# Where the decay weights and the rank rows of a gated linear attention are made, and which forward preparation comes first

## The chip, the cores and the metric

The kernel runs on one core of a Trainium2 chip, in one launch. The metric is the device time of the launch in microseconds (us). Five engines run their own instruction streams and meet at semaphores: PE (TensorE, matrix products and transposes), DVE (VectorE), ACT (ScalarE), POOL (GpSimd) and SP (SyncE, which here only issues transfers). An engine takes its instructions in the order in which they were written for it; an instruction whose input isn't there holds up all that stand behind it on that engine.

## The reference, cut to what matters

One encoder layer on 1024 tokens with 16 learned meta tokens ahead of them, width 1024. A combined projection feeds two groups of heads: a neighbourhood attention (16 heads of 64 over a 16 x 64 grid, window 8 x 16, meta tokens as extra keys) and a bidirectional gated linear attention (GLA; 4 heads, keys of 128, values of 256, decays per key from a projection of rank 16). Both are gated, put side by side and projected back onto the residual. What the change touches is the decay of the GLA and the meta tokens' part of its forward state:

```python
u = rmsnorm(concat([meta, x]), norm_g)                  # 1040 x 1024
gq, gk, gv, r_f, r_b, g_gate, nq, nk, nv, n_gate = split(u @ w_in)
lg_f = log_sigmoid(r_f @ w_decay_fwd + b_decay_fwd) / 16   # r_f, r_b: 1040 x 16
lg_b = log_sigmoid(r_b @ w_decay_bwd + b_decay_bwd) / 16   # w_decay: 16 x 512
G    = cumsum(lg) within a chunk
q_in, k_in, k_st = q * exp(G), k * exp(-G), k * exp(G_last - G)
U    = k_st^T v                 # per chunk and head: 128 x 256
S    = exp(G_last) * S + U      # state from chunk to chunk, in each direction
o    = tril(q_in k_in^T) v + q_in S
o_gla = rmsnorm(o_f + o_b) * silu(g_gate)
out  = x + concat([o_gla, neighbourhood_attention(...) * silu(n_gate)]) @ w_out
```

## The kernel before, in words

All matrix products that need it are made from three products of rounded halves (`mm3`, L411 to L413: high x high, low x high, high x low), so a dense projection shows as rows of L411, L412, L413 in turn. The channels of a weight row block (`raw`) are split into `wh` and `wl` by ACT, DVE and POOL ahead of PE.

The program is written out in one fixed order by a small planner, `Sched` (L69). It keeps an estimate of PE's time, `S.pe`. The main work is a generator that yields what it needs next: `("w", ns)` adds PE time, `("gap", ns)` fills that much estimated PE time with the next groups of the dense projections (`filler`), and `S.defer(ns, fn)` writes `fn`'s instructions once the estimate has advanced by ns. So a gap's length decides how many matmuls of dense work stand between two steps of the main work, and nothing is decided when the kernel runs.

There are two phases. First, eight head pairs of the neighbourhood attention, `attn(p)` for p = 0 to 7, some 69 us each; the filler brings the projections of the next pair and, late, `dense_gz(0)` and `dense_gv(0)` (queries, keys, values and rank columns of the first GLA head). In the trace `attn(2)` begins near 200 us and `attn(4)` near 338 us. Within `attn` the rows that matter here are: `Q` split into two halves (L731 by ACT, L738 by DVE, L742 by POOL), the scores `s` (L764, L765), softmax's maximum (L792) and exponentials (L798), its division `P` (L812 to L815), the transposes of `P` into `pp` (L826), their copies `PT` (L830 by ACT for the first head, L832 by DVE for the second) and the product with the values, `po` (L845). The natural-layout rows of the next pair come in between: squares and sums (`ss`, L552, by DVE), their inverse roots (`rstd`, L209 and L210, by POOL) and the scaled rows `nat` (L557, by DVE).

Then the attention's pool is closed, a pool `gp` is opened in its place, and the GLA begins: `gla_static()` (L995) reserves and loads constants, `r_prep()` (L917) turns the rank columns `rst` into rows, and `gla(h)` runs for the four heads, with the output gate `gg`, the next head's `gz` and `gv` and finally the output projection as filler. For each head the decays of the backward direction are made first (`decay_pe(1)`, product `pdec` at L1059, and on through ACT and DVE to `ga` and `gm`), then those of the forward direction; then the backward states run from chunk 7 to chunk 1 (transposed keys `pk` L1160, halves `kn` L1162 and L1163, products `pu`, states `SB` L1183 to L1186).

Three things are touched:

- **The decay weights `wd`**, one tile of 128 x 512 for each direction: rows 0 to 63 hold the rounded weights twice, rows 64 to 95 what the rounding left, rows 96 and 97 the bias in two halves, the rest zeros. The raw weights come by four transfers a direction into `wdst` (L1006, L1007); `wd_prep` (L1014) makes each tile by a memset on POOL and four operations on DVE (L1017 to L1021). Both directions are made in one piece in `r_prep`, after its first gap.
- **The rank rows `RS`**, 128 x 1040: transposes of `rst` on PE (`rt`, L929), six copies by ACT (L939), three subtractions by DVE (L941), and two memsets by POOL for the rows that meet the bias (L920, L921). `pdec` is `RS` times `wd`. Behind the three subtractions on DVE stand the evacuations of the gate's first two accumulation banks, `gt` from `pz_gg` (`gate_evac`, L484), which free the banks.
- **The forward preparations** (`fwd`, L1138): six steps that are written one by one behind the backward states of chunks `FWD_AT`: a cumulative sum over 1024 columns (`decay_scan`, L1080), its centring (`decay_mid`, L1088 to L1092), the meta tokens' key product (`ma`, the tile `mt`, L1141), exponentials and two products. The transpose of `ma` on PE, `pkt` (L1191), is written behind chunk 5.

## Time and profile before

| | |
|---|---|
| median of 3 runs | 1161.38 us (1160.01 to 1161.72) |
| the profiled execution's own time | 1161.92 us |
| its span, first to last instruction | 1159.1 us |
| PE busy | 1127.0 us, 97% of the span, 6739 matmuls |
| DVE busy | 771.6 us, 67%, 1965 instructions |
| ACT busy | 531.9 us, 46%, 1377 instructions |
| POOL busy | 300.8 us, 26%, 415 instructions |
| mean granted clock of TensorE | 0.997 |

How to read the rows: in the timeline, the first number is the start in us from the span's start, the second the duration, then engine, source line, operation, output and inputs with their shapes, and in square brackets the idle time just before and what ended it. In the list of waits, each row has an engine and the work that waited, what it waited for, and then the total in us, how many times, and the longest. In the table by stretches, each engine has its busy time and its number of instructions, followed by the granted clock of TensorE (1 is full), the mean busy share of the core's 16 transfer engines and GB/s. A stretch's matmuls are pipelined: a 512-column matmul lasts about 0.40 us in the record, and the next begins some 0.23 us after it began, so PE's pace is read from starts.

### The profile page before, as it was taken

The numbers are of one execution on the slowest core, as the hardware profiler recorded it, in microseconds if no ns is written. First come the engines' busy times: TensorE is split into PE (matmuls) and PEld (weight loads), VectorE is DVE, ScalarE is ACT, GpSimd is POOL, SyncE is SP. The second block draws the span as 40 slices with busy tenths as digits, with TensorE's granted clock in tenths as the row PEclk, the third lists the DMA queues.
The fourth block names the chain that finished last, engine by engine and source line by source line (L and its number), as shares of the span: only waits on it lengthen the run. The fifth ranks groups of instructions, "written<-read, shape, count | busy, mean of one in ns | idle before, by whom it ended". The sixth has DMA issues, their size and how long they took to land.

```text
span 1159.1 us, 18919 instructions
## 1 busy us (share of the span) xinstructions
PE 1127.0 (97%) x6739; PEld 981.4 (85%) x6739; DVE 771.6 (67%) x1965; ACT 531.9 (46%) x1377; POOL 300.8 (26%) x415
## 2 busy tenths in 40 slices
PE   8899999999999999999999799999999999999998
PEld 7789898998989889898898689879978977788886
DVE  6966767677677776767664676675486578656352
ACT  6756565664656555465553342542343244212120
POOL 3753534335353433624323001101100100000000
PEclk9999999999999999999999899999999999999999
DMA  7720402103030120402025312512522365314132
GB/s 248 231 74 2 126 2 85 43 2 125 1 124 4 55 73 2 127 2 85 21 65 160 108 35 74 151 38 78 149 61 61 84 195 185 106 50 132 47 113 104
DMA packets 74277, 99.34 MB, mean 86 GB/s; under 512 B 6532, under 2 KB 45188, under 8 KB 74184
## 3 DMA queue, kind: packets, MB, share of 16 engines
q1 hardware_dynamic: 69960, 89.76, 25.3%
q0 software_dynamic: 4224, 8.39, 2.5%
q8 instruction: 53, 0.87, 0.3%
q14 instruction: 40, 0.33, 0.1%
HBM read 72.89 MB, written 21.04 MB: 81 GB/s over the span
## 4 chain that ended last, share of the span: by engine, by line
PE 81%; DVE 9%; issue 4%; ACT 2%; DMA 2%; POOL 1%; SPq 0%; POOLq 0%; DVEq 0%; ACTq 0%
PE pn_na L411 7%; PE pn_na L412 6%; PE pn_na L413 6%; PE pout L412 5%; PE pout L411 5%; PE pout L413 5%; PE po L845 4%; PE pp L826 3%; PE pz_na L411 2%; PE pz_na L413 2%; PE pz_na L412 2%; PE pz_gz L411 2%; PE pz_gz L412 2%; PE pz_gz L413 2%; PE pn_gv L411 2%
## 5 line engine op out<-in xcount | busy, mean ns | idle before, releaser
L411 PE MATMUL pn_na<-wh,uh 128*128 128x384 f32 x512 | 180.5, 352 | 1.1 <-ACT uh L356 0.6
L412 PE MATMUL pn_na<-wl,uh 128*128 128x384 f32 x512 | 174.1, 340 | 1.1 <-POOL wl L255 0.9
L413 PE MATMUL pn_na<-wh,ul 128*128 128x384 f32 x512 | 173.4, 339 | 0.2
L209 POOL TENSOR_SCALAR post<-post 128x1 f32<-128x1 f32 x32 | 7.4, 230 | 391.7 <-ACT on L1211 336.8
L411 PEld LDWEIGHTS pn_na<-wh,uh 128*128 128x128 f32 x512 | 96.2, 188 | 10.2 <-issue 8.1
L411 PE MATMUL pout<-wh,oh 128*128 128x512 f32 x256 | 102.9, 402 | 0.1
L412 PE MATMUL pout<-wl,oh 128*128 128x512 f32 x256 | 101.6, 397 | 0.0
L413 PE MATMUL pout<-wh,oh 128*128 128x512 f32 x256 | 100.8, 394 | 0.0
L412 PEld LDWEIGHTS pn_na<-wl,uh 128*128 128x128 f32 x512 | 96.3, 188 | 3.4 <-POOL wl L255 2.2
L413 PEld LDWEIGHTS pn_na<-wh,ul 128*128 128x128 f32 x512 | 96.1, 188 | 1.2 <-DVE ul L358 1.1
L255 POOL TENSOR_TENSOR wl<-raw,wh 128x512 fp32r<-128x512 f32 (+2 forms) x63 | 82.1, 1322 | 44.2 <-PE pn_gv L412 27.5
L1335 DVE TENSOR_TENSOR acc<-acc,pout 128x512 f32<-128x512 f32 x64 | 43.8, 685 | 66.0 <-PE pout L413 66.0
L798 ACT ACTIVATE P<-P,sm 128x384 f32<-128x384 f32 x96 | 58.5, 609 | 51.9 <-DVE sm L795 51.9
L411 PE MATMUL pn_gv<-wh,uh 128*128 128x256 f32 (+1 forms) x256 | 76.3, 298 | 0.0
L413 PE MATMUL pn_gv<-wh,ul 128*128 128x256 f32 (+1 forms) x256 | 73.0, 285 | 0.0
L412 PE MATMUL pn_gv<-wl,uh 128*128 128x256 f32 (+1 forms) x256 | 72.9, 285 | 0.0
L210 POOL TENSOR_TENSOR ss<-ss,epsm 128x4 f32<-128x4 f32 x64 | 70.3, 1099 | 5.3
L792 DVE CUSTOM_DVE_ANT_0 P<-s,wt 128x416 f32<-128x416 f32 (+1 forms) x128 | 69.6, 544 | 2.5 <-PE s L765 2.5
L815 DVE TENSOR_SCALAR P<-P,sm 128x384 f32<-128x384 f32 (+1 forms) x128 | 66.9, 522 | 4.5
L252 DVE TENSOR_TENSOR wl<-raw,wh 128x512 fp32r<-128x512 f32 x63 | 43.0, 689 | 28.6 <-ACT wh L251 27.0
L832 DVE COPY PT<-pp 128x384 f32<-128x384 f32 (+1 forms) x80 | 36.3, 470 | 37.0 <-PE pp L826 36.5
L411 PE MATMUL pz_gg<-uh,wh 128*128 128x512 f32 x128 | 53.1, 415 | 7.3 <-DVE gt L484 7.3
(361 smaller groups left out, 2962.8 us busy)
## 6 DMA issues: line engine op xcount, KB each, us to landing
raw<-in_w_na_dram SPq DMA_DIRECT2D x56, 256.0 KB, 2.8
v_scr<-gvst SPq DMA_DIRECT2D x64, 128.0 KB, 2.3
raw<-in_w_o_dram SPq DMA_DIRECT2D x32, 256.0 KB, 3.1
oin<-o_scr SPq DMA_DIRECT2D x32, 256.0 KB, 3.0
v<-v_scr POOLq DMA_DIRECT2D x4, 1536.0 KB, 8.3
VM<-vnat SPq DMA_DIRECT2D x8, 512.0 KB, 4.7
o_scr<-ng SPq DMA_DIRECT2D x8, 512.0 KB, 3.5
raw<-in_w_gz_dram SPq DMA_DIRECT2D x16, 256.0 KB, 2.8
```

Source lines behind the costliest of these rows:

```text
L210: pool.tensor_tensor(dst, dst, epsm[: dst.shape[0], :eng_n], OP.pow)
L252: dve.tensor_tensor(wl[:, :n], r[:, :n], f32(wh[:, :n]), OP.subtract)
L255: pool.tensor_tensor(wl[:, :n], r[:, :n], f32(wh[:, :n]), OP.subtract)
L411: pe.matmul(ps, ah, bh, start=start, stop=False)
L412: pe.matmul(ps, ah, bl, start=False, stop=False)
L413: pe.matmul(ps, al, bh, start=False, stop=stop)
L792: dve.tensor_tensor_reduce(P[:, :n], ps[:, :n], wt[2 * p + a][:, off : off + n], 1.0, -3.0e38, OP.add, OP.max, mx)
L798: act.activation(loc, loc, AF.Exp, bias=mx, accum_out=sm[:, a : a + 1])
L815: dve.tensor_scalar(loc, loc, r, None, OP.mult)
L832: dve.tensor_copy(t[:w, e0:e1], pp[:w, e0:e1])
L845: pe.matmul(po[0][64 * a : 64 * a + 64, u4 * 128 : u4 * 128 + 128], V[:, 64 * a : 64 * a + 64], PT[a][:w, c * 128 : c * 128 + 128], start= ...
L1335: dve.tensor_tensor(a, a, ps, OP.add)
```

## The change

The two `wd` tiles and `RS` move from the pool `gp` to the pool `con`, which is open from the beginning, so that they can be written during the attention. The raw weights' tile `wdst` becomes a tile of the attention's pool with one buffer. Its four transfers for direction 0 are issued at the beginning of `attn(2)`, those for direction 1 at the beginning of `attn(4)`, and `wd_prep(d)` is deferred by 20000 ns of estimated PE time from there; one of its four DVE operations, the copy of the rounded rows, goes to ACT. The two memsets of `RS` are written ahead of `attn(6)`. The gaps of `r_prep` are shortened from 3662 and 8705 ns to 1200 and 2800 ns. In `fwd`, the meta tokens' key product comes first, behind chunk 7, and with it the cumulative sum stays behind chunk 7 and the centring behind chunk 6.

```diff
-R_NS = 8705.0
-R0_NS = 3662.0
+R_NS = 2800.0
+R0_NS = 1200.0
...
-FWD_AT = (7, 6, 6, 5, 4, 3)
+FWD_AT = (7, 7, 6, 5, 4, 3)
...
+WD_AT = (2, 4)
+WD_NS = 20000.0
...
-    def r_prep():
-
+    def r_static():
         RS = G["RS"]
         pool.memset(f32(RS[96:128]), 0.0)
         pool.memset(f32(RS[96:98]), -1.0)
+
+    def r_prep():
+
+        RS = G["RS"]
         yield ("gap", R0_NS)
-        wd_prep()
         pts = []
...
     def gla_static():
         gp = gpool[0]
-        G["wd"] = [gp.tile([128, 512], F32R, name=f"wd{d}") for d in range(2)]
-        G["RS"] = gp.tile([128, 1040], F32R, name="RS")
         G["hm"] = gp.tile([128, 8, 128], F32, name="hm")
...
-        G["wst"] = []
-        for d in range(2):
-            st = gp.tile([128, 1024], F32, tag="ga", name=f"wdst{d}", bufs=2)
-            for j in range(3):
-                sp.dma_start(st[32 * j : 32 * j + 32, 0:512], wdec[d])
-            sp.dma_start(st[96:98, 0:512], bdec[d : d + 1].to_broadcast([2, 512]))
-            G["wst"].append(st)
...
-    def wd_prep():
-        for d in range(2):
-            st, w = G["wst"][d], G["wd"][d]
-            pool.memset(f32(w[96:128]), 0.0)
-            dve.tensor_copy(w[0:98], st[0:98, 0:512])
-            dve.tensor_copy(st[64:98, 512:1024], f32(w[64:98]))
...
+    def wd_load(d):
+        st = nap.tile([128, 1024], F32, tag="wdst", name=f"wdst{d}", bufs=1)
+        for j in range(3):
+            sp.dma_start(st[32 * j : 32 * j + 32, 0:512], wdec[d])
+        sp.dma_start(st[96:98, 0:512], bdec[d : d + 1].to_broadcast([2, 512]))
+        G["wst"] = st
+
+    def wd_prep(d):
+
+        st, w = G["wst"], G["wd"][d]
+        pool.memset(f32(w[96:128]), 0.0)
+        dve.tensor_copy(w[0:98], st[0:98, 0:512])
+        act.activation(st[64:98, 512:1024], f32(w[64:98]), AF.Copy)
+        dve.tensor_tensor(w[64:96], st[64:96, 0:512], st[64:96, 512:1024], OP.subtract)
+        dve.scalar_tensor_tensor(
+            w[96:98], st[96:98, 512:1024], ident[96:98, 97:98], st[96:98, 0:512], OP.mult, OP.subtract
+        )
+
+    def decay_static():
+
+        G["wd"] = [con.tile([128, 512], F32R, name=f"wd{d}") for d in range(2)]
+        G["RS"] = con.tile([128, 1040], F32R, name="RS")
...
         fwd = [
+            lambda: dve.scalar_tensor_tensor(ma, ma, QSCALE, km[:, 0:16], OP.mult, OP.mult),
             lambda: decay_scan(0),
             lambda: decay_mid(0),
-            lambda: dve.scalar_tensor_tensor(ma, ma, QSCALE, km[:, 0:16], OP.mult, OP.mult),
...
+    decay_static()
     S.filler = fill_na()
     for p in range(NPAIR):
+        if p in WD_AT:
+            wd_load(WD_AT.index(p))
+            S.defer(WD_NS, lambda d=WD_AT.index(p): wd_prep(d))
+        if p == NPAIR - 2:
+            r_static()
         S.run(attn(p))
```

The order in which the instructions stand in the two programs, at three places. Rows have the source line, the operation, the output and the inputs with the program's names and numbers; in the changed program the same source stands 3 to 8 lines further down.

**DVE in the middle of `attn(2)`**, where the attention's softmax and the next pair's rows alternate. Before:

```order
L738 TENSOR_TENSOR Q_211_2636<-qt_1_2631,Q_11_98 64x256
L552 TENSOR_REDUCE ss_1_2672<-sq_1_2671 128x4
L832 COPY PT_2703<-pp_2699 128x384
L792 ISA P_2710,sm_2706<-s_2707,wt_1896 128x416
L792 ISA sm_2706 128x1
L795 TENSOR_SCALAR sm_2706<-sm_2706 128x1
```

and in the changed program:

```order
L741 TENSOR_TENSOR Q_211_2644<-qt_1_2639,Q_11_98 64x256
L555 TENSOR_REDUCE ss_1_2680<-sq_1_2679 128x4
L1021 CAST wd_137<-wdst_2459 98x512
L1023 TENSOR_TENSOR wd_137<-wdst_2459 32x512
L1024 SCALAR_TENSOR_TENSOR wd_137<-wdst_2459,ident 2x512
L835 COPY PT_2716<-pp_2712 128x384
L795 ISA P_2723,sm_2719<-s_2720,wt_1899 128x416
L795 ISA sm_2719 128x1
L798 TENSOR_SCALAR sm_2719<-sm_2719 128x1
```

Behind the sum `ss` and ahead of the copy `PT` now stand three operations of `wd_prep`. The first waits for a memset on POOL, the second for a copy on ACT. `attn(4)` has the same with `wd_138`. On POOL the memset stands behind the inverse root of that `ss`:

```order
L212 TENSOR_SCALAR ss_1_2680<-ss_1_2680 128x4
L213 TENSOR_TENSOR ss_1_2680<-ss_1_2680,epsm 128x4
L1020 MEMSET wd_137 32x512
L212 TENSOR_SCALAR ss_2_2764<-ss_2_2764 128x4
L213 TENSOR_TENSOR ss_2_2764<-ss_2_2764,epsm 128x4
```

**PE at the beginning of the GLA**, with the gate's product `pz_gg` as filler. Before:

```order
L411 MATMUL pz_gg_0_1_7570<-uh,wh_7030 128x512
L412 MATMUL pz_gg_0_1_7570<-ul,wh_7030 128x512
L413 MATMUL pz_gg_0_1_7570<-uh,wl_7031 128x512
L929 MATMUL rt_7584<-ident,rst 32x128 x4
L929 MATMUL rt_7589<-ident,rst 32x128 x4
L929 MATMUL rt_7594<-ident,rst 32x16
...
L411 MATMUL pz_gg_128_0_7637<-uh,wh_7451 128x512
L412 MATMUL pz_gg_128_0_7637<-ul,wh_7451 128x512
L413 MATMUL pz_gg_128_0_7637<-uh,wl_7452 128x512
L1059 MATMUL pdec_7658<-RS,wd_7532 128x512
L1059 MATMUL pdec_7661<-RS,wd_7532 128x512
L1113 MATMUL pdm_7655<-RS,wd_7531 128x16
```

and in the changed program:

```order
L414 MATMUL pz_gg_0_0_7564<-uh,wh_7055 128x512
L415 MATMUL pz_gg_0_0_7564<-ul,wh_7055 128x512
L416 MATMUL pz_gg_0_0_7564<-uh,wl_7056 128x512
L934 MATMUL rt_7571<-ident,rst 32x128 x4
L934 MATMUL rt_7576<-ident,rst 32x128 x4
L934 MATMUL rt_7581<-ident,rst 32x16
...
L414 MATMUL pz_gg_0_0_7564<-uh,wh_7491 128x512
L415 MATMUL pz_gg_0_0_7564<-ul,wh_7491 128x512
L416 MATMUL pz_gg_0_0_7564<-uh,wl_7492 128x512
L1067 MATMUL pdec_7616<-RS,wd_138 128x512
L1067 MATMUL pdec_7619<-RS,wd_138 128x512
L1121 MATMUL pdm_7613<-RS,wd_137 128x16
L414 MATMUL pz_gg_0_1_7601<-uh,wh_7055 128x512
```

The transposes `rt` now stand 6 matmuls after the first matmul of `pz_gg`, where 18 stood ahead of them, and `pdec` 15 matmuls after `rt`, where 42 stood between. In the changed program both banks of `pz_gg`'s first half are still being filled when `pdec` comes; before, they had been finished, and PE went on with the second half, whose banks are freed by L484.

**DVE in the backward states of head 1**, behind the state of chunk 7 (`SB`, L1186). Before:

```order
L1186 TENSOR_SCALAR SB_8752<-pu_8779,c_8673 128x256
L1080 SCALAR_TENSOR_TENSOR ga_8682<-hm,gm_8683 128x1024
L252 TENSOR_TENSOR wl_8789<-raw_8600,wh_8788 128x512
L484 TENSOR_TENSOR gt_8587<-pz_gg_128_1_8726,rbc 128x4x16x8
L252 TENSOR_TENSOR wl_8802<-raw_8639,wh_8801 128x512
L1163 TENSOR_TENSOR kn_8809<-pk_8807,kn_8809 128x128
L1183 TENSOR_TENSOR tb_8816<-pu_8812,SB_8752 128x256
L1184 TENSOR_SCALAR SB_8752<-tb_8816,c_8673 128x256
L1088 TENSOR_TENSOR gm_8683<-ga_8682 128x1024
L1090 COPY c_8820<-ga_8682 128x8
L1092 TENSOR_TENSOR c_8820<-c_8820,gm_8683 128x7
L1141 SCALAR_TENSOR_TENSOR mt_8615<-mt_8615,gkm_7886 128x16
```

and in the changed program:

```order
L1194 TENSOR_SCALAR SB_8752<-pu_8779,c_8673 128x256
L1147 SCALAR_TENSOR_TENSOR mt_8621<-mt_8621,gkm_7962 128x16
L1088 SCALAR_TENSOR_TENSOR ga_8682<-hm,gm_8683 128x1024
L255 TENSOR_TENSOR wl_8790<-raw_8603,wh_8789 128x512
L487 TENSOR_TENSOR gt_8588<-pz_gg_128_1_8726,rbc 128x4x16x8
L255 TENSOR_TENSOR wl_8803<-raw_8643,wh_8802 128x512
L1171 TENSOR_TENSOR kn_8810<-pk_8808,kn_8810 128x128
L1191 TENSOR_TENSOR tb_8817<-pu_8813,SB_8752 128x256
L1192 TENSOR_SCALAR SB_8752<-tb_8817,c_8673 128x256
L1096 TENSOR_TENSOR gm_8683<-ga_8682 128x1024
L1098 COPY c_8821<-ga_8682 128x8
L1100 TENSOR_TENSOR c_8821<-c_8821,gm_8683 128x7
```

The key product `mt` now stands ahead of the cumulative sum (`ga`, L1080 before) and of the centring (`gm`, L1088).

4 lines of the change are left out of this document (removed).

## The prediction

> **What bounds the kernel now.** I read the page first, then the list of what PE waited for, then the table by stretches and the timelines around the waits.
>
> ```profile
> PE 1127.0 (97%) x6739; PEld 981.4 (85%) x6739; DVE 771.6 (67%) x1965; ACT 531.9 (46%) x1377; POOL 300.8 (26%) x415
> PEclk9999999999999999999999899999999999999999
> ```
>
> PE is busy for 1127.0 of 1159.1 us. The change takes no matmul away, so it can win or lose only in the 32.1 us in which PE stands still, and in slices where its clock is below full: one slice shows an 8.
>
> ```profile
> PE pz_gg L411 <- DVE gt L484: 7.3, 2, 6.3
> PE pkt L1191 <- DVE mt L1141: 3.4, 4, 1.8
> PE pz_gz L411 <- DVE gt L484: 1.1, 1, 1.1
> ```
>
> The longest single wait, 6.30 us, is that of the gate's product for a bank that `gt` on DVE must empty. The transposes `pkt` wait four times, 3.4 us together. Both are places that the change touches. The stretches around the first:
>
> ```profile
> 636.20:642.40 6.20, 0.00 (x0) 0.00 (x0) 5.97 (x12) 0.00 (x0) 0.00 (x0) 0.89 1.11 326
> 642.40:648.00 5.60, 5.55 (x13) 4.39 (x14) 0.59 (x1) 0.00 (x0) 0.00 (x0) 0.51 0.12 39
> ```
>
> PE does nothing for one stretch while DVE is busy for 5.97 us of it. In the next its granted clock is 0.51, and 13 matmuls take 5.55 us. So the stall is paid for twice. The rows, of PE, then DVE, then ACT and SP:
>
> ```profile
> 623.55 0.39 PE L411 MATMUL pz_gg<-uh,wh 128*128 128x512 f32 x1
> 627.77 1.15 PE L929 MATMUL rt<-ident,rst 128*32 128x128 f32 x9
> 642.45 0.80 PE L411 MATMUL pz_gg<-uh,wh 128*128 128x512 f32 x1 [6.30 <-DVE gt L484]
> 647.74 0.70 PE L1059 MATMUL pdec<-RS,wd 128*128 128x512 f32 x2
> ...
> 627.60 1.65 DVE L258 TENSOR_TENSOR wl<-raw,wh 128x512 fp32r<-128x512 f32 x1
> 635.03 0.62 DVE L1018 CAST wd<-wdst 98x512 fp32r<-98x512 f32 x1 [5.78 <-DMA wdst<-in_wdec_dram]
> 640.32 1.36 DVE L941 TENSOR_TENSOR RS<-rt,RS 32x512 fp32r<-32x512 f32 x3
> 641.70 1.29 DVE L484 TENSOR_TENSOR gt<-pz_gg,rbc 128x512 f32<-128x512 f32 x2
> ...
> 625.11 0.29 ACT L973 ACTIVATE rst<-pn_gv,rs 128x32 f32<-128x32 f32 x1 [0.89 <-DVE gvst L971]
> 627.85 0.63 ACT L254 ACTIVATE wh<-raw 128x512 fp32r<-128x512 f32 x1 [0.90 <-DMA raw<-in_w_gv_dram]
> 629.01 2.27 ACT L939 ACTIVATE RS<-rt 32x512 fp32r<-32x512 f32 x6 [0.53 <-PE rt L929]
> ...
> 630.87 1.30 SPq L1006 DMA_DIRECT2D wdst<-in_wdec_dram  x3
> ```
>
> DVE waits 5.78 us for the raw decay weights, whose transfers begin only at 630.87. Then it makes both `wd` tiles from 635.03 until just ahead of 640.32, subtracts for `RS`, and only at 641.70 comes to the two evacuations that PE has waited for since 636.15.
>
> **The change part by part.** *Removed at the start of the GLA.* With `wd` made earlier, DVE goes from `wl` to the subtractions of `RS`, and in the changed order `pdec` comes before the first gate banks are full. So 6.30 goes. The half clock goes with it: from 623.55 to 627.77 there are 18 matmuls, 0.234 us each; from 642.45 to 647.74 there are 12 in 5.29 us, where 12 x 0.234 = 2.81 would do, so 2.48 was lost. The 1.12 before `pz_gz` is the same queue of evacuations a little later, behind decay work that now starts some 16 us earlier beside the same filler; I count it as gone. Sum removed: 6.30 + 2.48 + 1.12 = 9.90.
>
> *Added there.* PE gets to `rt` after 6 matmuls, 623.55 + 6 x 0.234 = 624.95; `rst` is there at 625.40. With 1.1 for `rt` (1.15 in its row, less the overlap of pipelined matmuls) and 15 matmuls, 3.5, PE would be at `pdec` at 629.55 if it never waited. `RS` is later: ACT has the `wh` of 627.85 ahead of the copies and is free at 628.48. Six copies took 2.27.
>
> ```profile
> L939 ACT ACTIVATE RS<-rt x6: 159/571/588, 629.0 to 631.1; 32x512 fp32r<-32x512 f32 x4, 32x16 fp32r<-32x16 f32 x2
> ```
>
> Big ones follow each other by about 0.5 and small ones by 0.15; the first subtraction, as the program is built, waits for the fourth copy, 628.48 + 0.5 + 0.5 + 0.15 + 0.57 = 630.2. The two large subtractions take 1.3 of the 1.36, so `RS` is ready at 631.5, and the waits at `rt` and `pdec` together are 631.5 - 629.55, about 2.0. Bounds: 0.5, if the copies come before that `wh`'s transfer lands late; 4.0, if one `wl` of 1.65 (627.60) gets ahead of the subtractions on DVE as well. Behind `pdec` on PE stands all filler, so PE pays the whole of it. I take 2.0, since ACT's row is the one that decides.
>
> *Does such a wait cost clock?* A wait of 2.20 in this trace did not:
>
> ```profile
> 58.62 0.46 PE L378 MATMUL rb<-dg,ones 128*128 128x128 f32 x2 [2.20 <-DVE dg L373]
> 59.15 0.40 PE L412 MATMUL pz_na<-ul,wh 128*128 128x512 f32 x1
> 59.38 0.40 PE L413 MATMUL pz_na<-uh,wl 128*128 128x512 f32 x1
> ```
>
> The pitch behind it is 0.23 at once. So the half rate begins somewhere between 2.20 and 6.30, and 2.0 costs only itself. In the Trainium skill, page "TensorE: Matmul & The Clock Gate", section "HAM oscillation — how this bites in real kernels", the rule is that gaps of PE beyond some 3.4 us bring the half rate back; the trace agrees on both sides, with 0.51 behind 6.30 and full pace behind 2.20. By that rule the forecast's waits cost no clock and the sum stands, and the 4.0 of the upper bound would cost it.
>
> *The key product first.* Head 1:
>
> ```profile
> 754.54 2.28 DVE L1080 TENSOR_TENSOR_SCAN ga<-hm,gm 128x1024 f32<-128x1024 f32 x1
> 760.86 0.17 DVE L1141 SCALAR_TENSOR_TENSOR mt<-mt,gkm 128x16 f32<-128x16 f32 x1
> 761.09 0.28 PE L1191 MATMUL pkt<-ident,mt 128*16 128x128 f32 x1 [1.84 <-DVE mt L1141]
> ```
>
> `mt` moves to where the cumulative sum now starts, 754.54, and is ready some 4.5 us before PE arrives, at 761.09 - 1.84 = 759.25. The cumulative sum moves back by 0.1 (0.17 less overlap), which nothing feels. What is late next behind `pkt`? The transposed keys' halves `kn` of the following chunk, on ACT and DVE; their product comes after at least two groups of filler, 6 x 0.234 = 1.4, and I see them just fit. So all of 3.4 goes.
>
> *Added in the attention, twice.* The tile's operations have these durations:
>
> ```profile
> L1017 POOL MEMSET wd<- x2: 520/520/520, 633.5 to 633.9; 32x512 f32 x2
> L1018 DVE CAST wd<-wdst x2: 426/522/618, 635.0 to 637.9; 98x512 fp32r<-98x512 f32 x2
> L1020 DVE TENSOR_TENSOR wd<-wdst x2: 682/682/683, 636.4 to 638.8; 32x512 fp32r<-32x512 f32 x2
> L1021 DVE SCALAR_TENSOR_TENSOR wd<-wdst,ident x2: 749/750/750, 637.1 to 639.5; 2x512 fp32r<-2x512 f32 x2
> ```
>
> They come in between these rows of `attn(2)`; the same rows, in the same spacing, stand in `attn(4)`:
>
> ```profile
> 221.60 0.42 DVE L552 TENSOR_REDUCE ss<-sq 128x4 f32<-128x256 f32 x1
> 223.01 0.56 DVE L832 COPY PT<-pp 128x384 f32<-128x384 f32 x1 [0.99 <-PE pp L826]
> 229.09 0.41 DVE L567 TENSOR_TENSOR kvm<-pm_na,kvt 16x256 f32<-16x256 f32 x1 [1.39 <-ACT kvt L566]
> 235.48 0.87 DVE L738 TENSOR_TENSOR Q<-qt,Q 64x256 fp32r<-64x256 f32 x2
> ...
> 222.45 1.01 POOL L210 TENSOR_TENSOR ss<-ss,epsm 128x4 f32<-128x4 f32 x1
> ...
> 225.77 0.66 PE L845 MATMUL po<-PT,vnat 128*64 128x128 f32 x8
> 226.26 0.39 PE L845 MATMUL po<-PT,VM 128*64 128x128 f32 x4
> 236.45 0.44 PE L764 MATMUL s<-K,Q 128*128 128x416 f32 x1
> ```
>
> DVE would be at the cast at 222.0, the end of `ss`. But the cast waits for POOL's memset, which stands behind the inverse root of 222.45: 223.46 + 0.52 = 224.0. Then cast 0.45, ACT's copy 0.57 (its nearest row is L939's 571 ns, at the same 512 columns) with DVE waiting for it, 0.68 and 0.75 with handovers: DVE is free at 226.6. Behind it are queued `PT`, the maxima, and all of softmax, 3.6 us late. `PT` ends at 227.2, and `po` was due at 225.77: PE waits 1.4. The next transposes `pp` lack their divided `P` by about 0.3, and at 236.45 `s` needs a `Q` that in the trace was ready 0.1 before, so some 0.6 more. DVE's own idle time, 1.39 us in one piece before 229.09, pays back the rest. That is 2.3 for each of the two, 4.6 together. Bounds for each: 0, if PE's filler groups cover the copy; 3.7, if DVE's whole delay reaches PE. I stay at the sum from rows, which lies between.
>
> The four transfers of each direction go ahead of the pair's own on SP, 1.30 for three and 0.33 for the fourth. The last of those, `VM`, is read first at 226.26:
>
> ```profile
> 206.48 0.57 SPq L680 DMA_DIRECT2D VM<-vm_scr  x1
> 481.30 0.67 POOL L718 TENSOR_SCALAR K<-K 64x576 fp32r<-64x576 f32 x1 [5.74 <-DVE K L708]
> ```
>
> It is issued 20 us before that and SP is free around it, so 1.63 costs nothing; without that cover it would cost 1.6. The two memsets of `RS`, 0.96 each where they stood, fit in POOL's 5.74 of idle time at the start of `attn(6)`: nothing; without it, 1.9 of POOL's time in front of `K`.
>
> *The rest.* With `pdec` 16 us earlier, the decay chain of head 0 meets other evacuations; between banks and `pk` I find gaps of some 0.3 to 1.0, and put 0.3 for small waits. More filler stands between the forward units of head 0, whose waits may shrink by up to 0.9; I put 0.4.
>
> **Sum**, against the profiled execution's 1161.92: - 9.90 - 3.43 + 2.0 + 4.6 + 0.3 - 0.4 = 1155.09. That execution was 0.54 above the median of the runs, 1161.38, so I expect a median of 1154.6, a ratio of 0.994.
>
> **The rivals.** Without any of the new waits the median would be 1147.95; each case adds its own.
>
> *The preparations hide.* If POOL reaches the memset sooner than its queue shows, or the stalled steps of softmax catch up within their own slack, neither `po` nor `s` waits. For it: 2.2 us lie between the end of `PT` (223.57) and `po` (225.77). Against it: the delay, 3.6, is larger. 1147.95 + 2.0 = 1150.0.
>
> *A new wait takes the old one's place.* `rt` to `pdec` has 15 matmuls, 3.5 us, for six copies, two subtractions and two handovers. If `RS` comes 4.0 late and the clock halves behind it: 1147.95 + 4.0 + 2.48 + 4.6 = 1159.0. Much the same, 1157.7, comes out if the waits at `pkt` aren't won, since the product behind them waits for `kn` instead. Against both: the rows above end sooner.
>
> *Slower.* One mechanism: DVE's stall in the attention reaches PE whole, and PE's clock falls behind it. The place is `po` behind `PT`; the price is 3.7 + 2.48 for each preparation, and with the same at `pdec`, 4.0 + 2.48: 1147.95 + 12.36 + 6.48 = 1166.8. It decides from waits of some length between 2.20, where the clock held, and 6.30, where it fell. For it: softmax, division and transposes all stand behind the stalled DVE. Against it: DVE has 1.39 us idle in a piece right after, and 2.2 of cover at `po`.
>
> **How the numbers follow.** My forecast, 1152.3 to 1157, has 0.58; the hidden preparations and anything faster 0.18; a new wait or an unwon `pkt`, 1157 to 1160, 0.20; the slower case 0.04. A range of 1150.5 to 1159.0 leaves out about a third of the second case, a quarter of the third and the last. About 0.2%, 2.3 us, can be told from no change here, so faster means below 1159.06. The first two cases and somewhat under half of the third give 0.84 for that; the rest of the third 0.12 for no difference; 0.04 for slower.
>
> **What would show it.** In the changed profile, the list of PE's waits should have no 6.3 at `pz_gg` and no `pkt`; the clock line should have no 8; `pdec` should first start near 631.5 with about 1.5 of idle time before it, and `rt` with 0.5. In both `attn(2)` and `attn(4)` DVE's cast should have an idle time of about 2 before it that POOL's memset ends, and PE a wait of 1 to 2 before `po`. If `po` shows no wait there, the hidden case is right; a `pdec` that waits for 3 or more with a slow stretch behind it makes it the second; a slow stretch in the attention the third. The forecast is wrong if PE's busy time and clock losses together don't fall by about 2.5, or its idle time by about 4.3.

## The result, and the profile after

| | before | changed |
|---|---|---|
| median | 1161.55 us (1160.01 to 1161.82, 4 runs) | 1147.71 us (1147.45 to 1148.64, 4 runs) |
| ratio | | 0.9886, 95% interval 0.9873 to 0.9899 |
| the profiled execution's own time | 1161.92 us | 1147.51 us |
| its span | 1159.1 us | 1145.7 us |

The change makes the kernel 13.8 us faster. I had forecast 6.8, so the sign was right and the size was about half of what came. The page of the changed kernel, busy times and granted clock:

```profile
PE 1122.2 (98%) x6739; PEld 976.7 (85%) x6739; DVE 769.9 (67%) x1963; ACT 533.5 (47%) x1379; POOL 300.7 (26%) x415
PEclk9999999999999999999999999999999999999999
```

The slice at 8 is gone. PE is busy for 4.9 us less with the same 6739 matmuls, and idle for 23.5 in place of 32.1. The list of what PE waited for:

```profile
PE pp L829 <- DVE P L818: 3.1, 6, 0.7
...
PE po L848 <- DVE PT L835: 2.2, 2, 1.1
PE pdec L1067 <- DVE RS L946: 1.4, 1, 1.4
...
PE pz_gg L414 <- DVE gt L487: 1.0, 1, 1.0
```

`pkt` and `pz_gz` are not in the list any more, and `pz_gg` has lost its wait of 6.3. Three rows are new or have changed their places: `po` in the two preparations, `pdec`, and `pp`. The beginning of the GLA, as a table by stretches and as a timeline of PE, DVE and ACT:

```profile
628.00:634.00 6.00, 4.56 (x19) 3.42 (x20) 3.56 (x5) 3.57 (x9) 5.94 (x6) 1.00 0.92 281
634.00:640.00 6.00, 6.00 (x27) 4.85 (x26) 3.06 (x4) 3.59 (x8) 0.99 (x2) 1.00 0.99 288
```

```profile
625.41 0.40 PE L414 MATMUL pz_gg<-uh,wh 128*128 128x512 f32 x1
626.81 1.15 PE L934 MATMUL rt<-ident,rst 128*32 128x128 f32 x9
633.11 0.72 PE L1067 MATMUL pdec<-RS,wd 128*128 128x512 f32 x2 [1.44 <-DVE RS L946]
...
631.78 1.36 DVE L946 TENSOR_TENSOR RS<-rt,RS 32x512 fp32r<-32x512 f32 x3 [0.69 <-ACT RS L944]
...
629.50 0.63 ACT L257 ACTIVATE wh<-raw 128x512 fp32r<-128x512 f32 x1 [1.01 <-DMA raw<-in_w_gv_dram]
630.04 2.25 ACT L944 ACTIVATE RS<-rt 32x512 fp32r<-32x512 f32 x6
```

Here the forecast's picture stands: six matmuls, `rt`, fifteen matmuls, then one wait at `pdec` for `RS`, which is late because ACT has a `wh` with a late transfer ahead of its copies. The wait is 1.44, where I had 2.0 for `rt` and `pdec` together; `rt` shows none. The granted clock stays at 1.00.

The first preparation in the attention, with rows of DVE, POOL and PE:

```profile
221.94 0.43 DVE L1021 CAST wd<-wdst 98x512 fp32r<-98x512 f32 x1 [2.05 <-POOL wd L1020]
223.06 0.68 DVE L1023 TENSOR_TENSOR wd<-wdst 32x512 fp32r<-32x512 f32 x1 [0.69 <-ACT wdst L1022]
224.54 0.56 DVE L835 COPY PT<-pp 128x384 f32<-128x384 f32 x1
...
221.38 0.52 POOL L1020 MEMSET wd<- 32x512 f32 x1
...
219.96 0.82 PE L829 MATMUL pp<-ident,P 128*128 128x128 f32 x6
225.15 0.54 PE L848 MATMUL po<-PT,vnat 128*64 128x128 f32 x5 [1.12 <-DVE PT L835]
229.18 0.52 PE L829 MATMUL pp<-ident,P 128*128 128x128 f32 x3 [0.31 <-DVE P L818]
236.53 0.52 PE L829 MATMUL pp<-ident,P 128*128 128x128 f32 x3 [0.34 <-DVE P L818]
242.60 0.82 PE L829 MATMUL pp<-ident,P 128*128 128x128 f32 x6
```

This too is as forecast: DVE waits 2.05 for POOL and 0.69 for ACT, `PT` comes late, and PE waits at `po` and twice at `pp`. The price is read from one `pp` to the third after it. The same place of the kernel before:

```profile
222.15 0.81 PE L826 MATMUL pp<-ident,P 128*128 128x128 f32 x6
242.01 0.82 PE L826 MATMUL pp<-ident,P 128*128 128x128 f32 x6
```

That is 19.86 before and 242.60 - 219.96 = 22.64 in the changed kernel, so 2.78 for the first preparation; the second, the same way, cost 2.47. Together 5.25, where I had 4.6. (Against the changed kernel's own pairs without a preparation, which take 19.75, it is 2.89 and 2.57.) Yet at 625.41 the GLA starts only 1.86 later than at 623.55 before. So some 3.4 us were won in the attention that no part of the forecast knew of, and the GLA itself, 535.55 us from its first matmul to the end of the span before and 520.29 now, won 15.3 where the forecast's terms make 11.4.

### The profile page after: what moved, and what is told of

Same layout as the page of the kernel before. It is cut to its first block, busy times and chain, and to the rows that moved or that the text cites. A ratio compares the mean times of both kernels' runs of the same rounds, so it can differ in the third digit from the quotient of the medians.

```text
span 1145.7 us, 18925 instructions
## 1 busy us (share of the span) xinstructions
PE 1122.2 (98%) x6739; PEld 976.7 (85%) x6739; DVE 769.9 (67%) x1963; ACT 533.5 (47%) x1379; POOL 300.7 (26%) x415
## 4 chain that ended last, share of the span: by engine, by line
PE 79%; DVE 7%; issue 5%; POOL 3%; ACT 3%; DMA 2%; SPq 0%; POOLq 0%; DVEq 0%; ACTq 0%
PE pn_na L414 6%; PE pn_na L416 5%; PE pn_na L415 5%; PE pout L414 5%; PE pout L416 5%; PE pout L415 5%; PE po L848 3%; PE pp L829 3%; PE pz_gz L414 3%; PE pz_gz L415 3%; PE pz_gz L416 3%; PE pz_gg L414 2%; PE pn_gv L414 2%; PE pz_gg L416 2%; PE pz_gg L415 2%
## 5 line engine op out<-in xcount | busy, mean ns | idle before, releaser
L254 ACT ACTIVATE wh<-raw 128x512 fp32r<-128x512 f32 x63 | 39.5, 630 | 48.7 <-PE pz_gz L415 20.4
L416 PEld LDWEIGHTS pout<-wh,oh 128*128 128x128 f32 x256 | 48.3, 189 | 11.6
```

Of the source, the lines that this page charges most:

```text
L254: act.activation(wh[:, :n], r[:, :n], AF.Copy)
L416: pe.matmul(ps, al, bh, start=False, stop=stop)
```

## The experiments

My theory from the changed profile: every edit does what the forecast said, and the missing microseconds come from parts of the attention that the edits don't touch. Its rivals: the edits help or hide each other, so that the parts don't add up; the preparations are hidden; or the gain comes from the decays' earlier start.

Ratios are to the kernel before on the same chip, with 95% intervals. The kernel before itself had medians from 1157.76 to 1161.56 in these sessions, so a difference of medians from two chips is softer than one of ratios. Where the text compares rows, they are of one profiled execution each.

### The key product alone, and all but the key product

```diff
-FWD_AT = (7, 6, 6, 5, 4, 3)
+FWD_AT = (7, 7, 6, 5, 4, 3)
         fwd = [
+            lambda: dve.scalar_tensor_tensor(ma, ma, QSCALE, km[:, 0:16], OP.mult, OP.mult),
             lambda: decay_scan(0),
             lambda: decay_mid(0),
-            lambda: dve.scalar_tensor_tensor(ma, ma, QSCALE, km[:, 0:16], OP.mult, OP.mult),
```

> The kernel before with nothing but the meta tokens' key product moved to the head of the forward preparations. Theory A (the waits of `pkt` are simply removed, and their short restart with them): the four waits, 0.30 + 1.84 + 0.99 + 0.30 = 3.4 us, go, some 0.15 more for each restart, so 1157.5 to 1158, ratio 0.9967. Rival (the product behind waits for the halves of the keys instead): within 1 us of before, with waits at `pu` in the list in place of those at `pkt`.

Measured: 1154.66 us, ratio 0.9966 (0.9951 to 0.9981); before took 1157.76 on that chip, so 3.1 less. No row of `pkt` is left in the list of waits, and at `pu` nothing new; one wait of 0.43 at `pz_gz` is new. So the waits at `pkt` are gone and not moved to the product behind.

The same lines taken out of the changed kernel:

> The changed kernel with the key product back in its old place. Theory A (parts add up): 3.4 to 3.9 us above the changed kernel, 1151.2 to 1151.6, the list of waits shows `pkt` at 3.4 again. Rival (the parts overlap, since an earlier decay leaves room): 1148 to 1149, and `pkt` waits for less than 1 us in all.

Measured: 1153.90 us, ratio 0.9967 (0.9953 to 0.9980). Of its waits:

```profile
PE pkt L1199 <- DVE mt L1149: 4.5, 4, 1.8
```

The four waits are 4.5 us in all, more than in the kernel before, since head 0's grew from 0.30 to 1.38 when its decays moved. So with the rest of the change in place, the key product's new place is worth 4.5 rather than 3.4. The run is 6.2 above the changed kernel's first median and 4.3 above its second (below), where I had expected 3.4 to 3.9; its profile also lost six of the meetings described below, and what each part made of the median is not shown.

### What a preparation costs: its memset moved away, and twice as many

```diff
     def decay_static():
         G["wd"] = [con.tile([128, 512], F32R, name=f"wd{d}") for d in range(2)]
         G["RS"] = con.tile([128, 1040], F32R, name="RS")
+        for d in range(2):
+            pool.memset(f32(G["wd"][d][96:128]), 0.0)
...
         st, w = G["wst"], G["wd"][d]
-        pool.memset(f32(w[96:128]), 0.0)
```

> The changed kernel with the two memsets of the decay weights' last rows written at the very beginning instead of ahead of each preparation, so that VectorE's cast waits for nothing on GpSimd. VectorE's stall there falls from 5.1 to about 3.0 us. Theory A (each preparation costs PE 2.5 to 2.8 us, since `PT`, `P` and the next `s` come late): the wait of 1.12 before `po` goes and those of 0.3 behind it shrink, each preparation costs 0.5 to 1, the time is 1143.5 to 1144.5. Rival (the preparations were hidden, and the 1.9 us that PE is later at the start of the GLA have another origin): no change beyond 1 us, 1147 to 1148.5.

Measured: 1143.56 us, ratio 0.9872 (0.9838 to 0.9906). DVE and PE in the first preparation:

```profile
221.56 0.42 DVE L1020 CAST wd<-wdst 98x512 fp32r<-98x512 f32 x1
...
221.71 0.82 PE L829 MATMUL pp<-ident,P 128*128 128x128 f32 x6
225.31 0.66 PE L848 MATMUL po<-PT,vnat 128*64 128x128 f32 x8
241.81 0.82 PE L829 MATMUL pp<-ident,P 128*128 128x128 f32 x6
```

The cast waits for nothing, `po` doesn't wait, and from `pp` to the third after it takes 20.10, in the second preparation too: a preparation now costs 0.24 in place of 2.8, or 0.35 in place of 2.9 against the changed kernel's own 19.75. So it was not DVE's own 1.9 us of work and the 0.69 at ACT that were dear, but the 2.05 us in which DVE stood behind POOL's queue. This rests on the rows; the ratio's interval overlaps the changed kernel's, 0.9873 to 0.9899.

```diff
-WD_AT = (2, 4)
+WD_AT = (2, 4, 3, 5)
...
-            wd_load(WD_AT.index(p))
-            S.defer(WD_NS, lambda d=WD_AT.index(p): wd_prep(d))
+            wd_load(WD_AT.index(p) % 2)
+            S.defer(WD_NS, lambda d=WD_AT.index(p) % 2: wd_prep(d))
```

> The changed kernel with each preparation of decay weights made twice, in the pairs 2 and 3, 4 and 5. Theory A (a preparation in the middle of a pair costs PE 2.5 to 2.8 us there, whatever else differs from run to run): from the transposes `pp` of one step to those three later, 19.85 us without a preparation, takes 22.3 to 22.6 in four pairs in place of two; the time is 5.2 above the changed kernel, ratio to before 0.993 to 0.994. Rival (the preparations lie in slack, and the later start of the GLA has another cause): within 1 us of the changed kernel, 0.989 to 0.990.

Measured: 1153.07 us, ratio 0.9951 (0.9932 to 0.9970), 3.5 above the second median of the changed kernel on the same chip, 1149.60, and in its profile the four pairs show 22.67, 22.36, 22.36 and 22.36. The second of them:

```profile
292.53 0.82 PE L829 MATMUL pp<-ident,P 128*128 128x128 f32 x6
314.89 0.81 PE L829 MATMUL pp<-ident,P 128*128 128x128 f32 x6
```

Each preparation costs PE 2.5 to 2.8 us in its pair, whatever else goes on. In the median the two more cost 3.5 rather than 5.2; the ratio's interval lies above the changed kernel's on this chip (0.9871 to 0.9918), so that the rival, no cost beyond 1 us, falls.

### Where DVE and POOL meet: the same kernels again, and one of the two held back

The waits of 0.66 at `pp` that the kernel before shows in the last step of six pairs, and the changed kernel in three, belong to no edit. DVE, POOL and PE near the first of them, in the kernel before:

```profile
122.18 1.82 DVE L258 TENSOR_TENSOR wl<-raw,wh 128x512 fp32r<-128x512 f32 x1
...
122.16 1.28 POOL L255 TENSOR_TENSOR wl<-raw,wh 128x512 fp32r<-128x512 f32 x1 [0.51 <-ACT wh L254]
...
125.43 0.52 PE L826 MATMUL pp<-ident,P 128*128 128x128 f32 x3 [0.66 <-DVE P L815]
```

and at the same place of the changed kernel, where PE has no wait:

```profile
121.44 0.69 DVE L261 TENSOR_TENSOR wl<-raw,wh 128x512 fp32r<-128x512 f32 x1
...
121.43 1.85 POOL L258 TENSOR_TENSOR wl<-raw,wh 128x512 fp32r<-128x512 f32 x1 [0.53 <-ACT wh L257]
```

Both engines begin a subtraction of the same shape within 0.02 us of each other; POOL's is the first of four. Either DVE takes 0.69 us and POOL's first 1.85, or POOL's takes 1.28 and DVE's 1.82. In the second case the division `P` that stands behind it on DVE is late, and so are PE's transposes. In the Trainium skill, page "SBUF — State Buffer", section "SBUF: two separate sides", an operation of DVE with two inputs and one of GpSimd share a port that the first to start holds for its whole instruction while the other blocks. The rows agree: DVE's 1.82 ends 0.56 us after POOL's 1.28, and POOL's 1.85 is 0.57 more than 1.28, both close to DVE's own 0.69. No run here shows the port itself.

> The kernel before, once more, for a second look at two things. Theory A: the first transposes of the last step of each pair wait 0.66 us because VectorE's subtraction for `wl` (about 122 us) and GpSimd's begin within 0.02 us of each other and VectorE's then takes 1.82 us instead of 0.69; who comes first is fixed by the program's own timing, so the same six of seven pairs show it again, and the time is within 0.15% of before. Rival: who comes first is chance; then other pairs show it than in the first profile, and the time moves by 0.7 us for each.

Measured: 1159.57 us, ratio 1.0010 (0.9994 to 1.0026), runs from 1157.01 to 1162.02. Its profile has the 1.82 in two pairs, the last two, not in six. So for this program it is chance who comes first. A pair of the kernel before takes 68.9 us where DVE loses and 68.4 where it wins, so a wait of 0.66 makes a pair 0.5 longer. The profiled execution of before that I predicted from, with six of seven lost, lay near the dear end. But the meetings are not all that differs from run to run: of the 42 runs of before that stand beside experiments on this chip, the 21 with a granted clock of 0.996 or more average 1156.8 us and the 15 with 0.994 or less 1160.3; how the clock comes to differ between executions is shown below, under the clock.

> The changed kernel once more. Theory A (chance decides, pair by pair, whether VectorE's or GpSimd's subtraction for `wl` gets through first, and each pair that VectorE loses costs PE about 0.65 us): the seven pairs show another pattern of 1.82 and 0.69 than in its first profile, the runs spread over 2 to 4 us, the ratio to before is 0.987 to 0.991. Rival (the pattern belongs to the program): the last three pairs lose again, as in the first profile, and the runs lie within 1 us.

Measured: 1149.60 us, ratio 0.9895 (0.9871 to 0.9918). DVE loses in two pairs, the second and the last, not in the last three. The runs lie within 0.9 us, where I had expected 2 to 4.

POOL held back by a short copy on ACT ahead of one `wh`:

```diff
+                if j >= 16 and key[0] == 'na' and j % 4 == 2:
+                    act.activation(tick, ident[:, 0:32], AF.Copy)
                 act.activation(wh[:, :n], r[:, :n], AF.Copy)
                 pool.tensor_tensor(wl[:, :n], r[:, :n], f32(wh[:, :n]), OP.subtract)
```

> The changed kernel with a copy of 32 columns on ScalarE ahead of the third of each four weight pieces in the pairs 1 to 7, so that GpSimd's subtraction starts some 0.2 us later and VectorE's always comes first. Theory A: VectorE's subtraction takes 0.69 in all seven pairs, no 0.7 us wait of `pp` is left, about 2 us below the changed kernel's mean on this chip and 4 to 5 below the run in which GpSimd is first. Rival (the waits of `pp` have another origin): the same number of them.

Measured: 1145.71 us, ratio 0.9864 (0.9836 to 0.9892). DVE held back by one on DVE:

```diff
                 dve.tensor_copy(wh[:, :n], r[:, :n])
+                if j >= 16 and key[0] == 'na':
+                    dve.tensor_copy(tick, ident[:, 0:32])
                 dve.tensor_tensor(wl[:, :n], r[:, :n], f32(wh[:, :n]), OP.subtract)
```

> The changed kernel with a copy of 32 columns on VectorE between its cast and its subtraction for `wl` in the pairs 1 to 7, so that GpSimd's subtraction always comes first. Theory A: VectorE's subtraction takes 1.6 to 1.8 in all seven pairs, each with a wait of 0.7 to 0.8 at `pp`, 4 to 5 us in all, 2 to 3 us above the changed kernel's mean. Rival: nothing but the copies' own 0.1 us.

Measured: 1149.67 us, ratio 0.9893 (0.9867 to 0.9919). So the first is 3.9 below the changed kernel on this chip, 1149.60, where about 2 was expected, and the second level with it, where 2 to 3 above was expected. Part of this offset lies in the GLA, which takes 518.7 us in the second kernel's profile and 522.5 in the changed kernel's second one: there `pdec` waited 2.04 with half clock behind it, in place of 1.52 at full clock. The tile of the extra copies also shifts the weights' tiles in both (below). The second pair in the profile of the first and then of the second kernel, DVE and POOL:

```profile
188.41 0.69 DVE L264 TENSOR_TENSOR wl<-raw,wh 128x512 fp32r<-128x512 f32 x1
188.50 5.99 POOL L261 TENSOR_TENSOR wl<-raw,wh 128x512 fp32r<-128x512 f32 x4 [0.61 <-ACT wh L260]
```

```profile
189.24 1.82 DVE L264 TENSOR_TENSOR wl<-raw,wh 128x512 fp32r<-128x512 f32 x1
189.22 5.70 POOL L259 TENSOR_TENSOR wl<-raw,wh 128x512 fp32r<-128x512 f32 x4 [0.51 <-ACT wh L258]
```

With POOL held back, DVE wins in the six pairs whose pieces the copy precedes and loses in the last, which it doesn't reach; with DVE held back, it loses in all seven. So what decides the meeting, and that it makes PE wait at `pp`, is shown, by holding back one side and then the other. The size is less sharp: between the two medians lie 4.0 us, between the two profiled executions 3.1, and from the first transposes of `q` to the last the two profiles differ by 3.4, about 0.55 for each of six pairs. What a pair loses is less than the wait of 0.66 to 0.73, since DVE and POOL meet once more some 5 us later: in five of the six pairs that DVE had won it then took 1.66 in place of 0.69, and in the same five PE waited 0.22 to 0.29 at `kt`; where DVE had lost the first meeting it took 0.69 at the second.

### The shorter gaps

```diff
-R_NS = 2800.0
-R0_NS = 1200.0
+R_NS = 8705.0
+R0_NS = 3662.0
```

> The changed kernel with the gaps of the rank rows' preparation back at 3662 and 8705 ns: the decay weights are ready early, but `rt` and `pdec` stand where they stood before. Theory A (the early decay weights take away the 6.3 us and the half clock, the shorter gaps only trade waits): no wait at `pdec`, none over 1.5 us at `pz_gg`, one of about 1.1 at `pz_gz`; within 1.5 us of the changed kernel, ratio to before 0.987 to 0.991. Rival (the gain comes from starting the decays earlier): 4 us or more above the changed kernel.

Measured: 1150.83 us, ratio 0.9906 (0.9881 to 0.9931), 1.2 above the changed kernel on the same chip, with intervals that overlap. No wait at `pdec` and none at the first gate banks; in their place

```profile
651.66 0.50 PE L414 MATMUL pz_gz<-uh,wh 128*128 128x512 f32 x1 [1.25 <-DVE gt L487]
```

and three smaller ones of 0.41, 0.59 and 0.19 in head 0. So the 6.3 us and the half clock go with the early decay weights alone; the gaps trade about 2.4 us of waits in head 0 for one of 1.4 to 2.0 at `pdec`.

### The clock behind a wait

Two, and in a second kernel four, additions on DVE ahead of the subtractions of `RS` make PE wait longer at `pdec`; their output is used by nothing.

```diff
+        lag = gpool[0].tile([128, 1024], F32, tag="gm", name="lag", bufs=2)
+        for _ in range(2):
+            dve.tensor_tensor(lag, rbc, rbc, OP.add)
         for q in range(3):
             dve.tensor_tensor(dst(1, q), src[q], f32(dst(0, q)), OP.subtract)
```

> The changed kernel with two additions of 128 x 1024 numbers on VectorE ahead of the subtractions of the rank rows, so that PE waits longer at `pdec`: 1.4 to 2.0 us become some 3.5 to 4.5. Theory A (the clock falls behind long idle times, and falls surely somewhere above 3 us): half pace behind it for 5 us, about 2.5 lost. Rival (only waits near 6 us cost clock): full pace from the first matmul on.

> As the run with two additions, with four: the wait at `pdec` becomes 6 to 7 us. Both theories: half pace behind it, 2 to 2.5 us lost, as behind the 6.30 us of the kernel before. If the loss grows with the wait, 3 or more.

Measured: 1153.15 and 1155.68 us, one run each. PE's wait and the stretches behind it, with two additions:

```profile
635.00 1.22 PE L1070 MATMUL pdec<-RS,wd 128*128 128x512 f32 x2 [4.27 <-DVE RS L949]
```

```profile
635.00:640.00 5.00, 5.00 (x12) 4.01 (x13) 0.03 (x1) 3.70 (x7) 0.00 (x0) 0.50 1.14 334
640.00:645.00 5.00, 5.00 (x20) 3.96 (x19) 3.35 (x4) 0.42 (x1) 0.00 (x0) 0.87 0.24 76
```

and with four:

```profile
637.86 1.22 PE L1070 MATMUL pdec<-RS,wd 128*128 128x512 f32 x2 [7.05 <-DVE RS L949]
```

```profile
637.86:642.00 4.14, 4.14 (x11) 3.32 (x12) 0.02 (x1) 3.20 (x5) 0.00 (x0) 0.53 1.03 322
```

Behind 4.27 us the half pace holds for some 6 us, behind 7.05 for 4. The loss does not grow with the wait. But it does not begin at one length either. The kernel before, at its second `pkt`, first in its first profile and then in its second:

```profile
761.09 0.28 PE L1191 MATMUL pkt<-ident,mt 128*16 128x128 f32 x1 [1.84 <-DVE mt L1141]
```

```profile
759.60 0.29 PE L1191 MATMUL pkt<-ident,mt 128*16 128x128 f32 x1 [1.84 <-DVE mt L1141]
```

The same wait of 1.84 was followed by full clock in the one and by half clock in the other. What differs is where the wait lies among fixed windows of 3.413 us. In all sixteen profiles the granted clock changes only at the edges of such windows: every stretch at full rate is a whole number of them long, and every stretch at half rate one or two, but for the last, which the end of the record cuts. Where the edges lie differs from execution to execution. Two windows around the wait, in the first profile and then in the second:

```profile
757.12:760.53 3.41, 2.12 (x11) 1.49 (x9) 3.38 (x7) 0.28 (x1) 0.00 (x0) 1.00 0.39 95
760.53:763.94 3.41, 2.85 (x15) 2.41 (x16) 1.38 (x8) 2.65 (x5) 0.00 (x0) 1.00 0.15 59
```

```profile
756.31:759.73 3.42, 1.58 (x10) 1.10 (x9) 3.35 (x11) 0.52 (x3) 0.00 (x0) 1.00 0.54 153
759.73:763.14 3.41, 3.41 (x10) 2.63 (x10) 0.70 (x3) 2.13 (x3) 0.00 (x0) 0.50 0.00 0
```

In the first, an edge cuts the wait into 1.29 and 0.56. In the second it lies whole within one window, PE is busy for only 1.58 us of that, and the whole next window runs at half rate, so that about half of it, 1.7 us, is lost. Leaving out the first 20 us and the cut end, the sixteen profiles have 17 windows at full rate in which PE stood still for 1.95 us or more, and half rate followed each of them. It followed only two of those with less: one with 1.84 (one with 1.87 stayed without), and one with 0.29 in which PE ran 16 matmuls of 48 or 16 columns, `pkm`. So it is not the length of a wait that decides but how little PE does within one window, and how an edge cuts a wait is chance: of three waits of 2.04 or 2.05 at `pdec`, the one that was cut into 1.16 and 0.89 kept the clock, and the two that lay in one window, but for 0.09 us, lost it. The waits of 4.27 and 7.05 each filled one window whole and brought two at half rate, of which the longer wait itself covers more.

So the bound between 2.20 and 6.30 that I had read from one profile was no bound. The very wait it was read from, 2.20 to 2.23 us at `rb` in each profile, is followed by half rate in nine of the sixteen, the changed kernel's first among them. The rule that the prediction drew on, gaps beyond some 3.4 us, is too coarse here, since 1.84 was enough. The Trainium skill, "TensorE: Matmul & The Clock Gate", section "What's actually happening", tells of a window of 3.4 us that runs freely of the kernel, and the windows of 3.413 us in these profiles agree. No run moved a wait against the windows on purpose; the executions did so by chance.

### Where the tiles lie

The kernel before, with nothing but this:

```diff
     def gla_static():
         gp = gpool[0]
-        G["wd"] = [gp.tile([128, 512], F32R, name=f"wd{d}") for d in range(2)]
-        G["RS"] = gp.tile([128, 1040], F32R, name="RS")
...
+    G["wd"] = [con.tile([128, 512], F32R, name=f"wd{d}") for d in range(2)]
+    G["RS"] = con.tile([128, 1040], F32R, name="RS")
     S.filler = fill_na()
```

> The kernel before with nothing but the two `wd` tiles and `RS` reserved in the constants' pool; all instructions in the order of before. The weights' tiles `wh` and `wl` then lie 8256 bytes further on in each partition. In the profiles so far the attention's 384-column matmuls follow each other by 0.1766 us in the three runs whose tiles lie as before and by 0.1741 in those whose tiles lie as in the change; a pair of heads without the 0.66 us wait takes 68.4 and 68.1 us. Theory A (where the tiles lie sets the pace): 0.174, pairs of 68.1 or 68.6, 2 to 3.5 us below before, ratio 0.997 to 0.998. Rival (the pace comes with the order of instructions or with the chip): 0.1766 and no difference in time.

Measured: 1159.36 us, ratio 1.0006 (0.9993 to 1.0019). Over the attention's longer rows of 384-column matmuls their starts are 0.1742 us apart on average, as in the changed kernel (0.1741), where before has 0.1766. One such row of 19 steps in the kernel before and in this one, first and last matmul:

```profile
280.00 0.34 PE L412 MATMUL pn_na<-wl,uh 128*128 128x384 f32 x1
...
283.36 0.34 PE L413 MATMUL pn_na<-wh,ul 128*128 128x384 f32 x1
```

```profile
277.32 0.34 PE L412 MATMUL pn_na<-wl,uh 128*128 128x384 f32 x1
...
280.62 0.34 PE L413 MATMUL pn_na<-wh,ul 128*128 128x384 f32 x1
```

3.36 us in the first, 3.30 in the second. The other operand, `uh` and `ul`, lies at the same place in both programs. So the pace comes with the place of the weights' tiles alone, and a pair in which DVE wins takes 68.1 us in place of 68.4. The time did not follow, though: the interval ends at 1.0019. In its profile DVE lost in five pairs, and the output projection's 512-column matmuls went the other way, from 0.2334 to 0.2342. Its runs also had less clock: 11 of 12 show 0.994 or less, of the 17 runs of before beside them 8, and these average 1158.9 against 1159.9. How much of the missing gain each of the three took is not shown. Theory A is right on the pace and wrong on the time.

The changed kernel with one more, unused, tile of 128 bytes ahead of the weights' tiles:

```diff
+    tick = con.tile([128, 32], F32, name="tick")
...
+    pool.memset(tick, 0.0)
```

> The changed kernel with one unused tile of 128 bytes a partition in the constants' pool, which moves the weights' tiles by 128 bytes more. Theory A (where the tiles lie sets the pace): the 512-column matmuls of the output projection go from 0.2342 to 0.2333, as in the two kernels that had such a tile for their extra copies, 0.7 to 1.2 us below the changed kernel in all. Rival (the extra copies set it): 0.2342.

Measured: 1149.80 us, ratio 0.9928 (0.9905 to 0.9951). The output projection's matmuls follow each other by 0.2333, against 0.2342 without the tile, as expected. Again the time didn't follow: DVE lost in all seven pairs of this profile. Its ratio lies above the changed kernel's first interval and overlaps the second, where 0.7 to 1.2 us less was expected. The pace with the place is shown; a gain in time from the place alone is not.

### The three edits together

The memsets at the beginning, the copy on ACT that holds POOL back (now for the pieces of every block), and the second gap at 4400 ns:

> The changed kernel with three edits: the decay weights' memsets at the beginning, the copy on ScalarE that lets VectorE's subtraction come first (now for the last pair as well), and the second gap of the rank rows' preparation at 4400 ns, so that 21 matmuls in place of 15 stand between `rt` and `pdec`. Theory A: preparations cost 0.3 us each in place of 2.6 (4.7 less), no wait of 0.7 at `pp` (about 2 less than on average), 1.4 less at `pdec`: 1139 to 1141 on a chip where before takes 1161, ratio 0.981 to 0.983. Rival (the edits meet the same slack): 0.985 to 0.987, as with one of them.

Measured: 1138.90 us (1138.75 to 1140.12, 5 runs), ratio 0.9829 (0.9812 to 0.9846). In its profile no wait of `pp` is left, nor of `po` in the attention, and

```profile
220.32 0.82 PE L832 MATMUL pp<-ident,P 128*128 128x128 f32 x6
240.33 0.82 PE L832 MATMUL pp<-ident,P 128*128 128x128 f32 x6
...
627.05 0.72 PE L1071 MATMUL pdec<-RS,wd 128*128 128x512 f32 x2 [0.25 <-DVE RS L949]
```

20.01 for a preparation's pair and 0.25 at `pdec`. The gains add up to what was expected: this kernel beats both the one before and the changed one, the latter by 8.8 to 10.7 us in the medians and by 6.6 to 7.7 in the ratios.

## Why the prediction was right and wrong, point by point

**What was removed at the start of the GLA: right.** 6.30, 2.48 and 1.12 went, as the list of waits and the table by stretches show.

**The new wait at `pdec`: right in place and cause**, 1.44 against 2.0; in other runs of the same order it was 1.3 to 2.05. That it cost no clock was luck: of three executions with 2.04 or 2.05, the length that I had forecast, two had half rate behind it.

**The key product: right on its own** (3.4 by the waits, 3.1 by the medians), though it does more inside the change, 4.5, since the moved decays would have made head 0's wait worse.

**The preparations: right in mechanism and nearly in size**, 5.25 against 4.6, and `memset_early` shows that POOL's queue is what made them dear. Of the parts, `po` waited 1.12 in place of 1.4; the 0.6 at `s` did not come, a second wait at `pp` came in its place.

**The sum was wrong by 7.6 us between the profiled executions** (1155.1 forecast, 1147.5 measured). The steps that failed:

- *"Sum, against the profiled execution's 1161.92"*: I took the one profiled execution of before as what the kernel does. It had lost the meeting of DVE and POOL in six pairs of seven, the changed kernel's in three: 1.5 us at 0.5 a pair. The rows stood in the page's list of waits, `pp` from `P` with 4.0 us in six waits, the second row of that list; I did not ask why seven equal pairs show six waits.
- *The edit of the pool, which I costed at nothing.* That the tiles' move shifts every weight tile by 8256 bytes, and PE's pace with it, was nowhere in the forecast. From the first transposes of `q` in the first pair to those in the last, the changed kernel took 2.3 us more, with 5.25 of preparations in it, so 2.95 less without them; 1.5 of these are the meetings', about 1.45 the pace's (1.65 if the preparations are counted against the changed kernel's own pairs).
- *"More filler stands between the forward units of head 0 ... I put 0.4", and 0.3 of new small waits*: the waits in the forward units of head 0, 0.60 at `po` and 0.25 behind it among them, went altogether, and no small ones came. Each removed wait also gives back some 0.15 more than its idle time, which I had left out: from the last `pu` to `pkt` it takes 0.12 without a wait and 0.58 with one of 0.30. Together that is about 1.7 us, an estimate. The rest of the GLA's 3.8 beyond forecast is 0.56 at `pdec`, about 0.8 of pace (an estimate from the average steps of its matmuls), and 0.7 at a wait for `ah` at the end of the GLA, 1.02 in the one profile and 0.32 in the other, which runs of the same order showed at anything from 0.16 to 1.00.
- *Outside the span*, 1.0 us less than before, and 0.5 at the start: nothing that the change touches, and luck. The profiled execution of before had 2.8 us outside its span, its second one 1.9, the changed kernel's 1.8 in both profiles.

The rival "the preparations hide" gave 1150.0, nearest to the result and for the wrong reason: they did not hide. "A new wait takes the old one's place" fell with 1.44 at full clock. "Slower" fell too, but one of my reasons against it was weak: a wait of 1.84 can cost clock. In the second rival the price of 1157.7 for the unwon `pkt` is a slip: the stated terms, 1154.6 and 3.43, give 1158.0. Neither sign of a wrong forecast came, since both asked only whether too little was won: PE's busy time fell by 4.9 and its idle time by 8.6. The chances by sign were right; the range, 1150.5 to 1159.0, was built around terms of edits alone and had no term for the execution that it started from.

## What to carry to other kernels

Before the sum, compare repeated parts of one profile with each other: where seven equal loops differ, the profile holds a coin toss, and a forecast needs its mean rather than that execution. An operation moved beside other work costs what it waits for, not what it takes; ask of each of its inputs which queue makes it, and write the cheap ones (here a memset) long ahead. A tile moved to another pool moves the addresses of all that is reserved behind it, so time such a move by itself. And a wait that cost no clock in one profile can cost it in the next: look at where it lies among the windows in which the granted clock changes, and at more than one execution, before a price of nothing goes into a sum.

## What the runs showed that I had not expected

- DVE's and POOL's subtractions of 128 x 512 that start within 0.02 us of each other take 0.69 or 1.82 us on DVE by chance, a wait of 0.66 to 0.73 for PE and about 0.5 us a pair; a copy of 32 columns ahead on one side settles it.
- PE's steps of 384 columns are 0.1766 or 0.1742 us by where the weight tiles lie, those of 512 columns in the output projection 0.2334 or 0.2342, with nothing else changed. In the built programs the first weight tile starts at byte 15680 of a partition before and at 23936 in the change; what in the address decides it was not tried.
- The granted clock changes only at the edges of windows of 3.413 us, which lie elsewhere in each execution, and half rate followed a window in which PE stood still for 1.95 us or more, 17 times of 17. So the same wait of 1.84 us was followed by full clock in one execution and by half rate in another, and the runs of before differ by some 3.5 us with the granted clock.
